# One transfer for the first tables, the last weights multiplied by the gate, and three idle products fewer in a two-layer hybrid kernel

## The chip, the cores and the metric

The kernel runs on one core of one Trainium2 chip. The metric is the device time of one execution in microseconds; a time stands for the median of several executions. The engines are named as the profile names them: PE (TensorE, matrix products; PEld are its weight loads), DVE (VectorE), ACT (ScalarE), POOL (GpSimd) and SP (SyncE, which issues most transfers). "ACTq" and "SPq" are transfers issued by ACT and SP.

## The reference

Two layers over 256 latent tokens of width 2048, with 256 context tokens as a prefix, all in fp32. The even layer mixes neighbourhood attention and a bidirectional Mamba-2 scan, the odd layer is a gated short convolution. Each layer modulates its normalised input by shift and scale and adds its output times a gate; the three come from the conditioning vector `c` (for the context rows from `c_ctx`) through `ada_w` and `ada_b`. Cut to what matters here:

```python
def adaln(cond, w, b):
    m = jax.nn.silu(cond) @ w + b
    return jnp.split(m, 3, axis=-1)                   # shift, scale, gate

def short_conv_mixer(h, w_in, conv_w, w_out):
    bg, cg, hv, g = jnp.split(h @ w_in, 4, axis=-1)
    return (jax.nn.silu(g) * (bg * dw_conv(cg * hv, conv_w))) @ w_out

for i in range(2):
    shift, scale, gate = adaln(c, ada_w[i], ada_b[i])
    h = rms_norm(x, norm_g[i]) * (1 + scale[:, None]) + shift[:, None]
    if i == 0:                                        # context rows too, with c_ctx
        y, _ = na_ssd_mixer(h, hc, ...)
    else:
        y = short_conv_mixer(h, sc_w_in[0], sc_conv_w[0], sc_w_out[0])
    x = x + gate[:, None] * y
return x
```

## The kernel before

**Numbers.** Every weight arrives in fp32 and is split into a high part (`split`: ACT copies it into an fp32r tile) and a low part (`low_part`: DVE subtracts the high part from the weight). A product of 128x128 by 128x512 is then three products: high by high, low by high, high by low. Activations are split in the same way (`hH`, `hL`; `y2` in the last product).

**Transfers.** A weight is a tile of 128x1024 (512 KB, `raw`), loaded by SP in the order of one list. `issue()` starts the next load when a `raw` buffer comes free. The small parameters lie in two tables, `small` and `const`, each with a first part (96 and 162 columns: conditioning vectors, norm weights and biases of layer 0; identity and a few constants) and a rest that is loaded later. ACT issues the two first parts at the program's start (L360, L362), ahead of everything else on its queue. SP issues the rows of `x` (L652), then the first weights of the modulation (L402).

**Order.** From about 60 us on, a planner sets the order by modelled times (`spawn`, `pump`, `force`: lists of tasks that yield until what they need is ready). The first part is another matter: `first()` holds a list of events, `at_(t, f)`, with times set by hand. The list is sorted by `t`, and its order is the order of the program on every engine.

**The head.** PE multiplies a tile of zeros (`warm(n, width)`, tile `tmp` at L204) while nothing is there to work on. ACT evaluates the tanh for SiLU of `c` and `c_ctx` (L548, `cth`), and ACT and DVE square the rows of `x` (L666, L668) for the norm. DVE and POOL make the factor (L640, L641), ACT and DVE scale the rows (L678), and PE turns the scaled rows (L209, `bank<-const,x`). Between them PE computes shift and scale of the first 256 channels: four products of 32x256 for each weight tile (`bank<-raw,cpad`, x8 in the profile, which counts two passes for a product in fp32; then `PT`, `xtm`, `yi`, which are spare places for weight tiles). `ada_copy` copies a result (`half`, L917), PE turns it (`bank<-const,half`), DVE makes `A` and `S` (L934, L936), ACT makes the modulated input `hH` (L1111), and the first product of the projections, that of K, follows (`bank<-w,hH`). Four idle products stand around the last pieces: `at_(18.97, warm, 1, 256)`, `at_(20.25, warm, 1, 256)`, `at_(20.72, warm, 1)` and `at_(20.73, warm, 1, 256)`. `r_turn` (`bank<-const,rx`) later turns the factors of the context rows, which arrive as `x<-in_cx`.

**The tail.** The last product is that of the odd layer, in four blocks of 512 columns. For each block `fin_gen` loads a row of the gate over all partitions (`tmp<-dram_mrow`), multiplies the result by it on DVE (L2575), adds the residual `x1` (L2578) and sends the block out (L2580). The last block is finished in three pieces, `LAST`: columns 0 to 256 of the second 128 tokens, then the first 128 tokens, then columns 256 to 512 of the second. The last six of its sixteen row blocks come from three weight tiles whose high and low parts lie in `KL`/`KL`, `QT`/`QL` and `wH`/`wL`; PE runs these six blocks piece by piece, after everything else.

Of the kernel before, what the change touches and what calls it, by code (L numbers as in the profile page):

```python
# [10 lines left out]
AF = mybir.ActivationFunctionType  # L11
# [4 lines left out]
KB = 16  # L16
# [4 lines left out]

_off = {}
_n = 0
for _name, _w in (("c", 16), ("cc", 16), ("g0", 16), ("ab0", 48), ("g1", 16), ("ab1", 48), ("cw", 160), ("cb", 32),
                  ("sg", 16), ("qg", 1), ("kg", 1), ("scw", 48), ("dtb", 1), ("alog", 1), ("dcol", 16)):
    _off[_name] = (_n, _n + _w)
    _n += _w
NSMALL, NFIRST = _n, 96
# [110 lines left out]


@with_exitstack
def kernel(ctx: ExitStack, tc, x, cx, ada0, w0, adaT, w_in, w_out, sc_in, sc_out, rpb, small, const,
                       strict, rows, scr, out):
    nc = tc.nc
    PS = bass.MemoryType.PSUM
# [9 lines left out]
    def st(shape, tag, dt=F32, name=None):  # L155
        return sb.tile(list(shape), dt, tag=tag, name=name or tag, bufs=1)
# [12 lines left out]
    WH = [t[:, :1024] for t in places]  # L169
    WL = [t[:, 1024:2048] for t in places]  # L170
    shifted = set()


    xrow = [st([128, D], "KT", name="x0")]
# [26 lines left out]
    def mm(o, l, r, start, stop):  # L201
        if start:
            bits[o.tensor.name] = o.shape[0] == 128 and o.shape[-1] == 512
        E(T.matmul(o, l, r, start=start, stop=stop, skip_group_check=True))  # L204
# [13 lines left out]
    def spawn(q, gen, tmps=0, halves=0, late=0):  # L218
        q.append(Task(gen, tmps, halves, late))
# [132 lines left out]
    def give(pool, *bs):  # L352
        pool.extend(bs)
# [2 lines left out]
    when = lambda f: ("if", f, 0)  # L356


    sm = st([128, NSMALL], "small")
    E(DMA2.dma_start(sm[:, :NFIRST], small[:, :NFIRST]))  # L360
    cs_ = st([128, NCONST], "const")
    E(DMA2.dma_start(cs_[:, :CFIRST], const[:, :CFIRST]))  # L362
# [59 lines left out]
    def split():  # L422
        k = pos["split"]
        raw, v = RAW.pop(k)
        nb, n = v.shape[1], v.shape[2]
        w = place()
        if n == 64:

            while lows:
                low_part()  # L430
            W = WH[w].rearrange("p (b c) -> p b c", b=nb)
            E(S.copy(W[:, :, :64], v))
            E(V.tensor_tensor(out=W[:, :, 64:], in0=v, in1=W[:, :, :64].bitcast(F32), op=ALU.subtract))
# [7 lines left out]
        E(S.copy(H, v))  # L441
        lows.append((k, H, Lo, v, raw))
        pos["split"] += 1
# [100 lines left out]
    zero = tmp()  # L544
    E(V.memset(zero, 0.0))
    E(V.memset(cpad, 0.0))
    cth = st([128, 32], "cth")
    E(S.activation(cth, sm[:, 0:32], AF.Tanh, scale=0.5))  # L548
    E(V.scalar_tensor_tensor(out=cth, in0=cth, scalar=1.0, in1=sm[:, 0:32], op0=ALU.add, op1=ALU.mult))
# [41 lines left out]
    for j in range(1, 7):  # L591
        q_w(j, 2)
        if j + 1 in DOTS:
            q_ada2(j + 1)
            q_dot(j + 1, 2)
            q_dot(j + 1, 3)
        else:
            q_ada(j + 1)
        q_w(j, 3)
        if j + 1 in DOTS:  # L600
            q_rowsA(j + 1)
        q_w(j, 4)
        if j == 3:
            loads.append(lambda: E(DMA.dma_start(sm[:, NFIRST:], small[:, NFIRST:])))
            loads.append(lambda: E(DMA.dma_start(cs_[:, CFIRST:], const[:, CFIRST:])))
        q_w(j + 1, 0)
        q_dot(j + 2, 0)
        q_w(j + 1, 1)
        q_dot(j + 2, 1)
# [113 lines left out]
    def chunk(kb0, kind, ps, first, last, lhs=None):  # L723

        H, Lo = use()
        nb = H.shape[1]
        for j in range(nb):
            kb = kb0 + j
            aH, aL = (hH[kb], hL[kb]) if lhs is None else lhs(kb)
            f, l = first and j == 0, last and j == nb - 1  # L730
            if kind == "act":
                mm_act(ps, aH, aL, H[:, j], Lo[:, j], f, l)
            else:
                mm_ws(ps, aH, aL, H[:, j], Lo[:, j], kind, f, l)
        used()
# [350 lines left out]
    def first():  # L1086
# [6 lines left out]
        def at_(t, f, *a):  # L1093
            ev.append((t + shift, len(ev), f, a))
# [1469 lines left out]
    def fin_gen(n, ps):  # L2564
        cols = slice(n * 512, (n + 1) * 512)
        yield when(lambda: n_back[0] >= 15)
        gb, os_ = tmp(), [tmp() for _ in range(2)]
        yield W_("SP", mrow[1:2])
        E(DMA.dma_start(gb, mrow[1, cols].partition_broadcast(128)))
        for t, c0, c1 in ((0, 0, 512), (1, 0, 512)) if n < 3 else LAST:  # L2570
            o = os_[t]
            c = slice(c0, c1)
            yield when(lambda: n < 3 or (3, t, c1) in at)
            yield W_("DVE", ps[t][:, c], gb)
            E(V.tensor_tensor(out=o[:, c], in0=ps[t][:, c], in1=gb[:, c], op=ALU.mult))  # L2575
            if c1 == 512:
                give(free_b, ps[t])
            E(V.tensor_tensor(out=o[:, c], in0=o[:, c], in1=x1[t][:, n * 512 + c0:n * 512 + c1], op=ALU.add))  # L2578
            yield W_("SP", o[:, c])
            E(DMA.dma_start(out[t * 128:(t + 1) * 128, n * 512 + c0:n * 512 + c1], o[:, c]))  # L2580
            if c1 == 512:
                give(free_t, o)
        give(free_t, gb)

    for n in range(4):
        if n == 1:
            force(lambda: n_back[0] >= 15, (urgent, back))
        ps = banks(2)
        for kb in range(0, KB if n < 3 else KB - 6, 2):
            force(lambda: y2[kb + 1] is not None)  # L2590
            chunk(kb, "act", ps, kb == 0, kb == KB - 2, lambda i: (y2[i][:, 0], y2[i][:, 1]))
        spawn(urgent, fin_gen(n, ps), 3)
# [12 lines left out]


_INS = ['x', 'cx', 'ada0', 'w0', 'adaT', 'w_in', 'w_out', 'sc_in', 'sc_out', 'rpb', 'small', 'const', 'strict', 'rows', 'scr']


# [73 lines left out]
```

## Time and profile before

| | us |
|---|---|
| median of 3 runs | 1724.89 |
| lowest, highest | 1723.09, 1725.05 |
| profiled execution, its own time | 1723.43 |
| its span | 1721.6 |

The span goes from the first to the last event of the profile; 1.8 us of the execution lie around it. The profile was taken from one execution on the one core, at a granted clock of 1.0. In rows of the timeline the numbers are the start and the duration in us; `x4` is a count; the bracket holds the idle time of the engine ahead of the row and what ended it. In rows of groups the numbers are the busy time in us and the mean of one instruction in ns.

### The profile page before, as it was taken

Reading aid. Unit: us, or ns where it says so; the run is one execution under the profiler, and the core shown is the slowest. Engines: PE = TensorE matmul, PEld = TensorE weight load, DVE = VectorE, ACT = ScalarE, POOL = GpSimd, SP = SyncE. Lnnn points to the kernel's source line nnn. Section 1 sums busy time; section 2 is a strip of 40 time slices with the busy share of each in tenths; the row PEclk is TensorE's granted clock in tenths of the full one; section 3 lists DMA queues with packets and bytes.
Section 4 is the critical chain, followed back from the end, with each engine's and each line's share of the span. In section 5 each row is a group of like instructions: output and inputs, shape, how many; then the busy total and the mean of one; then the engine's idle time right before and its main releaser. Section 6 shows DMA issues by size and latency. Waiting matters only on the chain.

```text
span 1721.6 us, 24689 instructions
## 1 busy us (share of the span) xinstructions
PE 1715.5 (100%) x9129; PEld 1449.9 (84%) x9129; DVE 1279.5 (74%) x2161; ACT 823.0 (48%) x1450; POOL 34.3 (2%) x28
## 2 busy tenths in 40 slices
PE   9999999999999999999999999999999999999999
PEld 5778899888889889889888898888888888888887
DVE  5699878877886778486877587887667767676754
ACT  6578464434553445244444244655444444444342
POOL 0000010000000000000001000000000000000000
PEclk9999999999999999999999999999999999999999
DMA  9988566456645675754775577767857788787863
GB/s 360 355 293 285 199 195 204 152 178 217 222 144 166 205 230 165 243 173 155 226 227 164 191 214 235 237 214 266 288 190 249 274 270 298 251 288 250 286 213 117
DMA packets 191368, 391.03 MB, mean 227 GB/s; under 512 B 16200, under 2 KB 45960, under 8 KB 190992
## 3 DMA queue, kind: packets, MB, share of 16 engines
q1 hardware_dynamic: 183936, 382.88, 67.2%
q10 hardware_dynamic: 7312, 6.59, 1.2%
q8 instruction: 71, 1.16, 0.3%
q14 instruction: 49, 0.40, 0.1%
HBM read 379.79 MB, written 9.62 MB: 226 GB/s over the span
## 4 chain that ended last, share of the span: by engine, by line
PE 99%; DMA 1%; DVE 0%; issue 0%
PE bank L204 96%; PE bank L209 3%; DMA raw<-in_ada 0%; DMA small<-in_small 0%; DVE tmp L2575 0%; DVE tmp L2578 0%
## 5 line engine op out<-in xcount | busy, mean ns | idle before, releaser
L441 ACT CAST w<-raw 128x1024 fp32r<-128x1024 f32 (+1 forms) x336 | 350.9, 1045 | 477.5 <-PE bank L204 389.2
L448 DVE TENSOR_TENSOR w<-raw,w 128x1024 fp32r<-128x1024 f32 (+1 forms) x336 | 406.9, 1215 | 215.0 <-ACT w L441 212.3
L204 PE MATMUL bank<-hH,w 128*128 128x256 f32 (+1 forms) x2064 | 486.5, 324 | 0.0
L204 PE MATMUL bank<-w,hH 128*128 128x512 f32 x1280 | 402.0, 394 | 0.0
L204 PEld LDWEIGHTS bank<-hH,w 128*128 128x128 f32 x2064 | 345.2, 188 | 32.1 <-issue 1.7
L204 PE MATMUL bank<-hL,w 128*128 128x256 f32 (+1 forms) x1040 | 334.7, 322 | 0.0
L204 PEld LDWEIGHTS bank<-w,hH 128*128 128x128 f32 x1280 | 236.9, 188 | 47.2 <-issue 0.8
L204 PE MATMUL bank<-w,hL 128*128 128x512 f32 x640 | 248.6, 391 | 0.0
L204 PEld LDWEIGHTS bank<-hL,w 128*128 128x128 f32 x1040 | 196.4, 189 | 14.5
L204 PE MATMUL bank<-w,h 128*128 128x512 f32 x768 | 178.5, 390 | 0.0
L204 PEld LDWEIGHTS bank<-w,h 128*128 128x128 f32 x768 | 144.0, 188 | 29.7
L842 DVE CUSTOM_DVE_ANT_0 raw<-raw,csb 128x1024 f32<-128x1024 f32 x128 | 155.3, 1219 | 10.5 <-DMA raw<-in_adaT 10.4
L204 PEld LDWEIGHTS bank<-w,hL 128*128 128x128 f32 x640 | 120.1, 188 | 25.3 <-DVE hL L1123 0.4
L204 PE MATMUL bank<-w,mix 128*128 128x512 f32 x588 | 138.4, 392 | 0.0
L204 PEld LDWEIGHTS bank<-w,mix 128*128 128x128 f32 x588 | 109.5, 188 | 22.0 <-issue 0.2
L204 PE MATMUL bank<-KL,h 128*128 128x512 f32 x264 | 63.6, 389 | 0.0
L1817 DVE SCALAR_TENSOR_TENSOR tmp<-bank,cwh,tmp 128x508 f32<-128x508 f32 (+1 forms) x80 | 59.4, 745 | 1.6
L204 PEld LDWEIGHTS bank<-KL,h 128*128 128x128 f32 x264 | 49.6, 188 | 10.3
L448 DVE TENSOR_TENSOR KL<-raw,KL 128x1024 fp32r<-128x1024 f32 x32 | 39.2, 1224 | 23.5 <-ACT KL L441 23.3
L204 PE MATMUL bank<-QT,h 128*128 128x512 f32 x168 | 55.8, 391 | 0.0
L204 PE MATMUL bank<-wH,h 128*128 128x512 f32 x168 | 55.3, 389 | 0.0
L441 ACT CAST QT<-raw 128x1024 fp32r<-128x1024 f32 x32 | 33.6, 1051 | 41.9 <-PE bank L204 34.5
(343 smaller groups left out, 2077.8 us busy)
## 6 DMA issues: line engine op xcount, KB each, us to landing
raw<-in_w_in SPq DMA_DIRECT2D x188, 512.0 KB, 3.7
raw<-in_adaT SPq DMA_DIRECT2D x128, 512.0 KB, 4.8
raw<-in_sc_in SPq DMA_DIRECT2D x128, 512.0 KB, 4.6
raw<-in_w_out SPq DMA_DIRECT2D x64, 512.0 KB, 4.6
raw<-in_ada SPq DMA_DIRECT2D x39, 512.0 KB, 6.2
raw<-in_sc_out SPq DMA_DIRECT2D x32, 512.0 KB, 4.5
tmp<-dram_csr SPq DMA_DIRECT2D x32, 256.0 KB, 5.8
raw<-in_w SPq DMA_DIRECT2D x15, 512.0 KB, 5.9
```

The source lines that it names most:

```text
L204: E(T.matmul(o, l, r, start=start, stop=stop, skip_group_check=True))
L209: E(T.transpose(o, i, ident if k == 128 else ident[:k, :k]))
L441: E(S.copy(H, v))
L448: E(V.tensor_tensor(out=Lo, in0=v, in1=H.bitcast(F32), op=ALU.subtract))
L842: E(V.tensor_tensor_reduce(out=raw, in0=raw, in1=csb, scale=1.0, scalar=0.0, op0=ALU.mult, op1=ALU.add, accum_out=gp[:, h, m:m + 1]))
L1817: E(V.scalar_tensor_tensor(out=do, in0=di, scalar=cwh[:, 32 * k + ch:32 * k + ch + 1], in1=do, op0=ALU.mult, op1=ALU.add))
```

## The change

There are three parts.

1. The two tables become one input, `tables`, ordered so that the two first parts lie side by side: 128 rows of 258 columns, 1032 bytes each, in place of 128 rows of 384 and 128 of 648 bytes. ACT issues that one transfer. Ahead of it ACT now runs a tanh on a tile of zeros, `cth`, which DVE clears first; the load of the function table stands in front of that tanh.
2. The gate of the last 512 columns is loaded once, ahead of the last three blocks of the loop (`gate3`). DVE multiplies the last three weight tiles by it, in place, before they are split. The last six row blocks then go into banks of their own (`last`) rather than on top of the ten before. `fin_gen` finishes the ten (gate and residual) as it finishes other blocks, and adds the banks of `last` piece by piece, with one addition for each.
3. Three of the four idle products around 20 us are left out; the 512 wide one stays.

```diff
+    tab = st([128, NSMALL + NCONST], "tables")
+    cth = st([128, 32], "cth")
+    sm, cs_ = tab[:, :NSMALL], tab[:, NSMALL:]
+    T0, T1 = NSMALL - NFIRST, NSMALL + CFIRST
+    E(V.memset(cth, 0.0))
+    E(S.activation(cth, cth, AF.Tanh))
+    E(DMA2.dma_start(tab[:, T0:T1], tables[:, T0:T1]))
-    sm = st([128, NSMALL], "small")
-    E(DMA2.dma_start(sm[:, :NFIRST], small[:, :NFIRST]))
-    cs_ = st([128, NCONST], "const")
-    E(DMA2.dma_start(cs_[:, :CFIRST], const[:, :CFIRST]))
...
+        if k >= nw[0] - 3:
+            E(V.tensor_tensor(out=v, in0=v, in1=gate3[0].unsqueeze(1).to_broadcast([128, 2, 512]), op=ALU.mult))
         E(S.copy(H, v))
...
-        at_(18.97, warm, 1, 256)
-        at_(20.25, warm, 1, 256)
         at_(20.72, warm, 1)
-        at_(20.73, warm, 1, 256)
...
+        for t in range(2):
             o = os_[t]
+            yield W_("DVE", ps[t], gb)
+            E(V.tensor_tensor(out=o, in0=ps[t], in1=gb, op=ALU.mult))
+            give(free_b, ps[t])
+            E(V.tensor_tensor(out=o, in0=o, in1=x1[t][:, cols], op=ALU.add))
+            if n < 3:
+                yield W_("SP", o)
+                E(DMA.dma_start(out[t * 128:(t + 1) * 128, cols], o))
...
+        for t, c0, c1 in LAST:
+            o, c = os_[t], slice(c0, c1)
+            yield when(lambda: (3, t, c1) in at)
+            yield W_("DVE", last[t][:, c], o)
+            E(V.tensor_tensor(out=o[:, c], in0=last[t][:, c], in1=o[:, c], op=ALU.add))
             yield W_("SP", o[:, c])
             E(DMA.dma_start(out[t * 128:(t + 1) * 128, n * 512 + c0:n * 512 + c1], o[:, c]))
...
         if n == 1:
             force(lambda: n_back[0] >= 15, (urgent, back))
+            force(lambda: budget[0] >= 1)
+            budget[0] -= 1
+            gate3.append(tmp())
+            E(DMA.dma_start(gate3[0], mrow[1, 1536:2048].partition_broadcast(128)))
...
+    last = banks(2)
     ws = [use(q) for q in range(3)]
     for t, c0, c1 in LAST:
         for q, (H, Lo) in enumerate(ws):
             for b in range(2):
                 hl = y2[KB - 6 + 2 * q + b]
                 for a_, w_ in ((0, H), (0, Lo), (1, H)):
-                    mm(ps[t][:, c0:c1], hl[:, a_, t * 128:(t + 1) * 128], w_[:, b, c0:c1], False, q == 2 and b == 1 and a_ == 1)
+                    st_ = q == 0 and b == 0 and a_ == 0 and w_ is H and c0 == 0
+                    mm(last[t][:, c0:c1], hl[:, a_, t * 128:(t + 1) * 128], w_[:, b, c0:c1], st_, q == 2 and b == 1 and a_ == 1)
```

What stands on the engines at the places that this moves follows, in the program's order. A name with a number is a tile, `[waits ...]` the semaphores that the instruction waits for.

On ACT, the program's first instructions before:

```order
L360 DMA small<-in_small 128x96
L362 DMA const<-in_const 128x162
L548 ACT_TABLE_LOAD
L548 ACTIVATE cth<-small 128x32 [waits DMAHW0_49]
L666 ACTIVATE tmp_66,ssq<-x_98 128x512 [waits DMAHW1_49]
```

and after:

```order
L365 ACT_TABLE_LOAD
L365 ACTIVATE cth<-cth 128x32 [waits DVE_49]
L366 DMA tables<-in_tables 128x258
L554 ACTIVATE cth<-tables 128x32 [waits DMAHW2_49,Activation_49]
L672 ACTIVATE tmp_66,ssq<-x_98 128x512 [waits DMAHW0_49]
```

The transfer has moved from the head of the queue to a place behind the table load and an activation that waits for DVE, and the activation on the tables waits for one transfer that holds both.

On PE, around the last pieces of the modulation (`xtm`, `yi`) and the first product of K, before:

```order
L204 MATMUL bank_86<-xtm,cpad 32x256 [waits DMAHW4_49]
L204 MATMUL bank_86<-xtm,cpad 32x256 x3
L204 MATMUL bank_84<-tmp_65 128x256 [waits DVE_49]
L204 MATMUL bank_86<-yi,cpad 32x256 [waits DMAHW5_49]
L204 MATMUL bank_86<-yi,cpad 32x256 x3
L204 MATMUL bank_85<-tmp_65 128x256 [waits DVE_49]
L209 MATMUL bank_86<-const,half_75 128x128 [waits Activation_49]
L209 MATMUL bank_86<-const,half_75 128x128
L204 MATMUL bank_87<-tmp_65 128x512 [waits DVE_49]
L204 MATMUL bank_88<-tmp_65 128x256 [waits DVE_49]
L204 MATMUL bank_89<-w_95,hH_308 128x512 [waits Activation_49]
```

and after:

```order
L205 MATMUL bank_86<-xtm,cpad 32x256 [waits DMAHW3_49]
L205 MATMUL bank_86<-xtm,cpad 32x256 x3
L205 MATMUL bank_86<-yi,cpad 32x256 [waits DMAHW4_49]
L205 MATMUL bank_86<-yi,cpad 32x256 x3
L210 MATMUL bank_86<-tables,half_75 128x128 [waits Activation_49]
L210 MATMUL bank_86<-tables,half_75 128x128
L205 MATMUL bank_84<-tmp_65 128x512 [waits DVE_49]
L205 MATMUL bank_85<-w_95,hH_305 128x512 [waits Activation_49]
```

The three idle products of 256 columns (`tmp_65` is the tile of zeros) are gone; the products on `yi` follow directly on those on `xtm`.

On DVE, the program's last instructions before (L448 is the low part of a weight, L2575 the gate, L2578 the residual):

```order
L448 TENSOR_TENSOR QL<-raw_91,QT 128x1024 [waits DMAHW7_49,Activation_49]
L448 TENSOR_TENSOR wL_9836<-raw_93,wH_9835 128x1024 [waits DMAHW0_49,Activation_49]
L2575 TENSOR_TENSOR tmp_71<-bank_82,tmp_66 128x256 [waits DMAHW4_49,PE_49]
L2578 TENSOR_TENSOR tmp_71<-tmp_71,x1b 128x256 [waits DVE_49]
L2575 TENSOR_TENSOR tmp_69<-bank_89,tmp_66 128x512 [waits PE_49]
L2578 TENSOR_TENSOR tmp_69<-tmp_69,x1a 128x512 [waits DVE_49]
L2575 TENSOR_TENSOR tmp_71<-bank_82,tmp_66 128x256 [waits PE_49]
L2578 TENSOR_TENSOR tmp_71<-tmp_71,x1b 128x256 [waits DVE_49]
```

and after (L446 is the multiplication of a weight by the gate, L454 the low part, L2578 the gate, L2580 the residual, L2592 the addition of a piece of the last six blocks):

```order
L446 TENSOR_TENSOR raw_91<-raw_91,tmp_65 128x1024 [waits DMAHW7_49]
L446 TENSOR_TENSOR raw_93<-raw_93,tmp_65 128x1024 [waits DMAHW0_49]
L454 TENSOR_TENSOR QL<-raw_91,QT 128x1024 [waits Activation_49]
L454 TENSOR_TENSOR wL_9833<-raw_93,wH_9832 128x1024 [waits Activation_49]
L2578 TENSOR_TENSOR tmp_69<-bank_85,tmp_65 128x512 [waits PE_49]
L2580 TENSOR_TENSOR tmp_69<-tmp_69,x1a 128x512 [waits DVE_49]
L2578 TENSOR_TENSOR tmp_71<-bank_82,tmp_65 128x512 [waits PE_49]
L2580 TENSOR_TENSOR tmp_71<-tmp_71,x1b 128x512 [waits DVE_49]
L2592 TENSOR_TENSOR tmp_71<-bank_86,tmp_71 128x256 [waits DVE_49,PE_49]
L2592 TENSOR_TENSOR tmp_69<-bank_87,tmp_69 128x512 [waits PE_49]
L2592 TENSOR_TENSOR tmp_71<-bank_86,tmp_71 128x256 [waits PE_49]
```

The multiplications by the gate stand ahead of the splits of the last weights, the first tile's a few rows earlier; behind the last product of PE one operation is left where two were.

More of the change, by code (lines that the diff above doesn't have):

```diff
@@ L23 @@
 _n = 0
-for _name, _w in (("c", 16), ("cc", 16), ("g0", 16), ("ab0", 48), ("g1", 16), ("ab1", 48), ("cw", 160), ("cb", 32),
-                  ("sg", 16), ("qg", 1), ("kg", 1), ("scw", 48), ("dtb", 1), ("alog", 1), ("dcol", 16)):
+for _name, _w in (("g1", 16), ("ab1", 48), ("cw", 160), ("cb", 32), ("sg", 16), ("qg", 1), ("kg", 1), ("scw", 48),
+                  ("dtb", 1), ("alog", 1), ("dcol", 16), ("c", 16), ("cc", 16), ("g0", 16), ("ab0", 48)):
     _off[_name] = (_n, _n + _w)
@@ L141, with kernel @@
 @with_exitstack
-def kernel(ctx: ExitStack, tc, x, cx, ada0, w0, adaT, w_in, w_out, sc_in, sc_out, rpb, small, const,
+def kernel(ctx: ExitStack, tc, x, cx, ada0, w0, adaT, w_in, w_out, sc_in, sc_out, rpb, tables,
                        strict, rows, scr, out):
@@ L171 @@
     shifted = set()
+    gate3 = []
     xrow = [st([128, D], "KT", name="x0")]
@@ L546 @@
     E(V.memset(cpad, 0.0))
-    cth = st([128, 32], "cth")
-    E(S.activation(cth, sm[:, 0:32], AF.Tanh, scale=0.5))
-    E(V.scalar_tensor_tensor(out=cth, in0=cth, scalar=1.0, in1=sm[:, 0:32], op0=ALU.add, op1=ALU.mult))
+    both = sm[:, _off["c"][0]:_off["cc"][1]]
+    E(S.activation(cth, both, AF.Tanh, scale=0.5))
+    E(V.scalar_tensor_tensor(out=cth, in0=cth, scalar=1.0, in1=both, op0=ALU.add, op1=ALU.mult))
     csil = st([128, 32], "csil")
@@ L603 @@
         if j == 3:
-            loads.append(lambda: E(DMA.dma_start(sm[:, NFIRST:], small[:, NFIRST:])))
-            loads.append(lambda: E(DMA.dma_start(cs_[:, CFIRST:], const[:, CFIRST:])))
+            loads.append(lambda: E(DMA.dma_start(tab[:, :T0], tables[:, :T0])))
+            loads.append(lambda: E(DMA.dma_start(tab[:, T1:], tables[:, T1:])))
         q_w(j + 1, 0)
@@ L2566, in fin_gen @@
         yield when(lambda: n_back[0] >= 15)
[L2567 to L2570, printed above, removed]
-            o = os_[t]
[L2572 to L2578, printed above, removed]
+        gb = tmp() if n < 3 else gate3[0]
+        os_ = [tmp() for _ in range(2)]
+        if n < 3:
+            yield W_("SP", mrow[1:2])
+            E(DMA.dma_start(gb, mrow[1, cols].partition_broadcast(128)))
+        for t in range(2):
+            o = os_[t]
+            yield W_("DVE", ps[t], gb)
+            E(V.tensor_tensor(out=o, in0=ps[t], in1=gb, op=ALU.mult))
+            give(free_b, ps[t])
+            E(V.tensor_tensor(out=o, in0=o, in1=x1[t][:, cols], op=ALU.add))
+            if n < 3:
+                yield W_("SP", o)
+                E(DMA.dma_start(out[t * 128:(t + 1) * 128, cols], o))
+                give(free_t, o)
+        if n < 3:
+            give(free_t, gb)
+            return
+        for t, c0, c1 in LAST:
[3 more added lines that the diff above has]
+            E(V.tensor_tensor(out=o[:, c], in0=last[t][:, c], in1=o[:, c], op=ALU.add))
             yield W_("SP", o[:, c])
             E(DMA.dma_start(out[t * 128:(t + 1) * 128, n * 512 + c0:n * 512 + c1], o[:, c]))
-            if c1 == 512:
-                give(free_t, o)
-        give(free_t, gb)
     for n in range(4):
@@ L2587 @@
             force(lambda: n_back[0] >= 15, (urgent, back))
+            force(lambda: budget[0] >= 1)
+            budget[0] -= 1
+            gate3.append(tmp())
+            E(DMA.dma_start(gate3[0], mrow[1, 1536:2048].partition_broadcast(128)))
         ps = banks(2)
-        for kb in range(0, KB if n < 3 else KB - 6, 2):
+        k1 = KB if n < 3 else KB - 6
+        for kb in range(0, k1, 2):
             force(lambda: y2[kb + 1] is not None)
-            chunk(kb, "act", ps, kb == 0, kb == KB - 2, lambda i: (y2[i][:, 0], y2[i][:, 1]))
-        spawn(urgent, fin_gen(n, ps), 3)
+            chunk(kb, "act", ps, kb == 0, kb == k1 - 2, lambda i: (y2[i][:, 0], y2[i][:, 1]))
+        spawn(urgent, fin_gen(n, ps), 3 if n < 3 else 2)
+    last = banks(2)
     ws = [use(q) for q in range(3)]
@@ L2604 @@
     force(lambda: not urgent, (urgent,))
-_INS = ['x', 'cx', 'ada0', 'w0', 'adaT', 'w_in', 'w_out', 'sc_in', 'sc_out', 'rpb', 'small', 'const', 'strict', 'rows', 'scr']
+_INS = ['x', 'cx', 'ada0', 'w0', 'adaT', 'w_in', 'w_out', 'sc_in', 'sc_out', 'rpb', 'tables', 'strict', 'rows', 'scr']
 def kernel(**inputs):
@@ L2668 @@
         'w_out': f('na_ssd_w_out')[0], 'sc_in': f('sc_w_in')[0], 'sc_out': f('sc_w_out')[0], 'rpb': table,
-        'small': small, 'const': const, 'strict': strict,
+        'tables': np.concatenate([small, const], axis=1), 'strict': strict,
         'rows': np.concatenate([f('ssd_dt_bias')[0].reshape(1, 64), f('ssd_a_log')[0].reshape(1, 64)], axis=1),
```

7 lines of the change are left out of this document (3 added, 4 removed).

## The prediction

> **What bounds the kernel now.** I read the page first: the busy times, the clock row and the chain that ended last. Then the list of everything that TensorE (PE) waited for.
>
> ```profile
> PE 1715.5 (100%) x9129; PEld 1449.9 (84%) x9129; DVE 1279.5 (74%) x2161; ACT 823.0 (48%) x1450; POOL 34.3 (2%) x28
> ...
> PEclk9999999999999999999999999999999999999999
> ...
> PE 99%; DMA 1%; DVE 0%; issue 0%
> ```
>
> ```profile
> PE bank L204 <- DVE tmp L545: 1.5, 1, 1.5
> PE bank L204 <- DVE rx L640: 1.0, 1, 1.0
> ```
>
> PE is busy for 1715.5 of 1721.6 us, at full clock in every slice, and 99% of the chain is PE. Its only waits that the list shows are 1.5 us for the first zero tile and 1.0 us ahead of its first real product. All of that is over by 11 us. From there PE works without a break, so time taken from or given to PE in the head is carried to the end, unless a later input holds PE at a fixed time. Two places can therefore matter: the head, up to about 35 us, and what comes after the last product. Everything between is the same rows in the same order, with PE as its limit.
>
> **The tail: one operation instead of two behind the last product.** These rows of the timeline are the end of the program and what lies ahead of it (start, duration, engine, what, and in brackets the idle time before it and who ended it).
>
> ```profile
> 1702.53 1.23 DVE L448 TENSOR_TENSOR wL<-raw,wH 128x1024 fp32r<-128x1024 f32 x1 [1.24 <-ACT wH L441]
> ...
> 1709.41 0.88 PE L204 MATMUL bank<-KL,y 128*128 128x256 f32 x6
> ...
> 1711.76 0.42 DVE L2575 TENSOR_TENSOR tmp<-bank,tmp 128x256 f32<-128x256 f32 x1 [8.00 <-PE bank L204]
> ...
> 1717.70 0.28 PE L204 MATMUL bank<-wH,y 128*128 128x256 f32 x1
> 1718.02 0.42 DVE L2575 TENSOR_TENSOR tmp<-bank,tmp 128x256 f32<-128x256 f32 x1 [0.73 <-PE bank L204]
> 1718.47 0.43 DVE L2578 TENSOR_TENSOR tmp<-tmp,x1b 128x256 f32<-128x256 f32 x1
> ```
>
> Before, the last product ends at 1717.98, the multiplication by the gate starts at 1718.02, the addition at 1718.47, and the output leaves behind it. Afterwards one addition of the same 128x256 stands there, since the gate is in the weights and the sum so far already lies in SBUF. What goes is the step from one start to the next, 1718.47 - 1718.02 = **0.45 us**. What is late next is the same product of PE, so nothing takes the operation's place.
>
> What pays for it: three multiplications of 128x1024 on DVE, each priced by the low part of the same shape, 1.23 us; and two full-width pairs on the banks as they stand before the last six blocks (four operations of 128x512, some 0.7 us each, between the 0.42 of 128x256 and the 1.23 of 128x1024). DVE has been idle for 8.00 us ahead of 1711.76. The multiplications, 3 x 1.23 = 3.7 us, go into that hole and delay the casts behind them: per block at most the multiplication and the low part waiting behind it. The last low part starts at 1702.53 before, and PE takes the first of these blocks at 1709.41, 5.6 us after 1703.76. With all 3.7 us in a row ahead of the last block, 1.9 us are still left. The four partial operations start when PE closes the earlier blocks, at about 1709.6, take 2.9 us and end near 1712.6, while the last product is 5 us later. I cost all of this at **nothing**. Without that cover it would cost up to 3.7 us. The gate row is now loaded once, earlier, on SP's queue, 40 us ahead of its use; the load of 256 KB is the same one, moved.
>
> **The head: three idle products.** First the transfer on which the next real product waits (issue, KB, median us to landing), then the timeline from the first idle product on.
>
> ```profile
> yi<-in_ada SPq DMA_DIRECT2D x1, 512.0 KB, 10.2
> ```
>
> ```profile
> 9.36 0.33 SPq L402 DMA_DIRECT2D yi<-in_ada  x1
> ...
> 18.95 0.64 PE L204 MATMUL bank<-xtm,cpad 128*32 128x256 f32 x8
> 19.52 0.70 PE L204 MATMUL bank<-tmp 128*128 128x256 f32 x2
> 20.15 0.64 PE L204 MATMUL bank<-yi,cpad 128*32 128x256 f32 x8
> ...
> 20.85 0.37 ACT L917 COPY half<-bank 128x256 f32<-128x256 f32 x1 [1.43 <-PE bank L204]
> ...
> 21.28 0.44 PE L209 MATMUL bank<-const,half 128*128 128x128 f32 x2
> 21.55 1.46 PE L204 MATMUL bank<-tmp 128*128 128x512 f32 x4
> ...
> 22.29 1.09 ACT L1111 ACTIVATE hH<-xm,S,A 128x256 fp32r<-128x256 f32 x2 [0.54 <-DVE S L936]
> ...
> 22.94 0.74 PE L204 MATMUL bank<-w,hH 128*128 128x512 f32 x2
> ...
> 33.00 0.32 PE L209 MATMUL bank<-const,rx 128*128 128x128 f32 x1
> ```
>
> The first idle product stands at 19.52 and holds back the products on yi until 20.15, 0.63 us. yi lands at 9.36 + 10.2 = 19.56. Without the idle product they start at about 19.6, 0.5 us earlier. The second one, behind yi's products, hides: the turn at 21.28 waits for ScalarE's copy of the bank (20.85 + 0.37 = 21.22) in any case. The third hides in the same way with the part of the row at 21.55 that is left: the first product of K at 22.94 needs hH, whose ACT row starts at 22.29. So the copy, the turn, S, hH and the first product of K move by 0.5 us together, to about 22.4, and two of the three products bring nothing of their own.
>
> How much of the 0.5 us is left further on? DVE squares a quarter of the context rows, which come with the DMA stream and do not move:
>
> ```profile
> 24.72 0.68 DVE L668 CUSTOM_DVE_ANT_0 tmp<-x 128x512 f32<-128x512 f32 x1
> 25.33 0.69 DVE L469 TENSOR_TENSOR w<-PT,w 128x512 fp32r<-128x512 f32 x1
> 28.51 0.69 DVE L668 CUSTOM_DVE_ANT_0 tmp<-x 128x512 f32<-128x512 f32 x1 [0.29 <-DMA x<-in_cx]
> ```
>
> The low half of K at 25.33 stands behind that square and so can move by little; 28.51 waits for the stream outright, and the turn at 33.00 is a fixed time later, behind DVE's and GpSimd's work on those sums. K's low product, and then 33.00, take back what PE was ahead by. Its bounds are 0 (everything taken back) and -0.5 us (nothing). I take **-0.2 us**, nearer to 0, since the row at 28.51 shows that the chain to 33.00 hangs on the transfer.
>
> **The tables as one transfer.** Here the trace does not show the new thing: a DMA issued by ScalarE (ACT) behind its table load.
>
> ```profile
> 0.73 0.41 ACTq L360 DMA_DIRECT2D small<-in_small  x1
> ...
> 1.17 0.46 ACTq L362 DMA_DIRECT2D const<-in_const  x1
> ...
> 1.67 1.28 ACT L548 ACT_TABLE_LOAD   x1 [1.67 <-PEq L2672]
> ...
> 5.10 0.23 ACT L548 ACTIVATE cth<-small 128x32 f32<-128x32 f32 x1 [2.15 <-DMA small<-in_small]
> ...
> 8.09 0.69 DVE L668 CUSTOM_DVE_ANT_0 tmp<-x 128x512 f32<-128x512 f32 x1 [0.29 <-DMA x<-in_x]
> ...
> 11.31 1.33 ACT L678 ACTIVATE x<-x,rx 128x512 f32<-128x512 f32 x2 [0.61 <-POOL rx L641]
> ...
> 12.53 0.66 PE L209 MATMUL bank<-const,x 128*128 128x128 f32 x4
> ```
>
> ```profile
> 288.92 1.05 ACT L441 CAST w<-raw 128x1024 fp32r<-128x1024 f32 x1 [1.39 <-issue]
> 288.94 0.79 ACTq L1801 DMA_DIRECT2D dram_csr<-tmp  x2
> ```
>
> The table load costs 1.28 us and hides before and after; the small activation on zeros adds 0.23. What can cost time is the landing. small is issued at 0.73 and lands 4.37 us later, when the activation at 5.10 starts. If ACT's sequencer issues past a running operation, as at 288.94 under the cast of 288.92, tables leave at about 1.1 and land near 1.1 + 4.37 = 5.5, 0.4 late. If the load and the activation block it, they leave at 0.73 + 1.28 + 0.23 = 2.24 and land near 6.6, 1.5 late. What queues behind: ACT's first squares stand behind the activation that waits for tables, and so do DVE's, behind the two operations on cth; the scaled rows of the second block and their turn on PE stand behind those. There is room: 0.29 us of idle time ahead of DVE's square at 8.09, and the scaled quarter is done at 11.31 + 0.67 = 11.98, 0.55 ahead of its turn at 12.53. So 0.84 us are free. The delays are **0** for a landing 0.4 late and 1.5 - 0.84 = 0.66 us for one 1.5 late, and that falls on the stretch that has just lost a 0.63 us idle product: the head gain goes first. Below nothing there is a little too: the rows of x share the engines with one queue of 128 pieces less. The two transfers hold 48 + 81 KB, which at 512 KB in 1.27 us (raw tiles: PE took two of them at 11.96 and 13.23) is 0.3 us of bytes; I bound the gain at 0.2. I take 0, nearest to the row at 288.94.
>
> ```profile
> 11.96 0.64 PE L204 MATMUL bank<-raw,cpad 128*32 128x256 f32 x8
> ...
> 13.23 0.64 PE L204 MATMUL bank<-raw,cpad 128*32 128x256 f32 x8
> ```
>
> The Trainium skill, in "ScalarE: Activation LUTs", section "What ACT_TABLE_LOAD costs", speaks against this part: it gives about 1283 ns for the load, which the row at 1.67 bears out, and about 1380 ns of drain behind it, 2.66 us in all. The trace of before cannot show the drain, since the activation behind the load waits for small until 5.10. By that page the tables would leave at 0.73 + 2.66 = 3.4 us; the term would then be about +1.8 rather than 0 (an estimate from that page's figure, with small's 4.37 us to landing).
>
> **Sum.** Tail -0.45, head -0.2, tables 0: **-0.65 us**, bounds -0.45 - 0.5 - 0.2 = -1.15 and, with the head gain lost, -0.45. On the profiled execution that is 1723.43 - 0.65 = 1722.8. The median of the runs shown is 1724.89, 1.46 above that execution, and the runs spread over 2 us; put on the median, it is **1724.2**.
>
> **Rivals.**
> - *The tables land late and hold PE* (the slower side). Place: the turn at 12.53. Point: a landing more than 0.84 us after 5.10. For it: no row shows an issue behind a table load. Against it: 288.94. With the landing 1.5 late the 0.66 us eat the 0.63 of the idle product and the rest is the tail, 1724.4. Slower than before it becomes from a landing about 1.9 late on (0.84 + 0.63 + 0.45). If the operation behind the load starts only after a pause as long as the load (1.28 more), the landing is 2.8 late: 2.8 - 1.9 = +0.9 us, 1725.8. The skill's drain, named above, is of that kind.
> - *PE falls back to its slow start.* The windows of the head show what that is:
>
> ```profile
> 0.00:7.40 7.40, 5.95 (x7) 2.53 (x8) 2.89 (x11) 2.85 (x6) 0.20 (x4) 1.00 0.69 232
> 7.40:10.70 3.30, 2.40 (x6) 0.76 (x4) 2.73 (x10) 2.61 (x6) 0.55 (x1) 1.00 1.02 416
> ```
>
>   One pass of the same idle product (fp32 takes two) is 5.95 / 7 = 0.85 us up to 7.4 and 2.40 / 6 = 0.40 behind it. If the thinner work between 19.5 and 22.9 sent PE back for as long a stretch, seven passes would lose 0.45 us each, 3.1 us, and with the tail 1724.89 + 3.1 - 0.65 = 1727.3. Against it: PE stood still for 1.0 us (the list of waits) before its first real product, and those at 11.96 then took the same 0.64 as at 18.95. The new gaps are near 0.4 and 0.5 us, and a 512-wide idle product stays between them. The Trainium skill, "TensorE: Matmul & The Clock Gate", Part 1, puts the return to half speed behind an idle window of about 3.4 us; by it the loss would be none here, and 1.7 us if it came.
> - *It does not do what it says in the head*: K's low half and the turn at 33.00 take back all, so -0.45 alone, 1724.4.
> - *The stream runs ahead*: nothing is taken back and x lands earlier, -1.15, 1723.7.
>
> **Chances and range.** Forecast 0.50, nothing left in the head 0.20, late tables 0.17, stream ahead 0.10, slow PE 0.03. The range: the lowest run with the lower bound, 1723.09 - 1.15 = 1721.9, and the highest run with the late tables, 1725.05 + 0.9 = 1725.9. About 0.2%, 3.4 us, is what a measurement of this kernel can tell from no change; no case but a long slow stretch or a shifted run reaches it: faster 0.02, same 0.95, slower 0.03.
>
> **What would show it.** Right: in the timeline's tail one operation between the last product and the output, with the start of the second one gone; the products on yi at about 19.6 with no idle product ahead; the first product of K near 22.4; the turn that stood at 33.00 within 0.5 us of it; the DMA row of tables at 1.1 and the first activation on it before 5.9. Wrong: the activation on tables after 6.0 with the turn of 12.53 later than that; PE waits for KL, QT or wH at the end, which would mean that the multiplications are not hidden; passes of 512 columns above 0.8 us after 20 us; or a span that differs by more than 3 us, which none of these terms could give.

## The result, and the profile after

| | us |
|---|---|
| median after (4 runs) | 1761.46 (1760.65 to 1762.46) |
| median before, all runs beside them (4) | 1724.22 |
| ratio | 1.0215, 95% interval 1.0203 to 1.0228 |
| profiled execution after, its own time and span | 1760.65, 1758.9 |

The change makes the kernel slower by 37 us. The forecast was 0.7 faster, and none of its cases reached this. The page of the changed kernel answers to the first lines of the prediction, and the list of PE's waits to the second fence:

```profile
PE 1751.5 (100%) x9123; PEld 1451.2 (83%) x9123; DVE 1284.5 (73%) x2166; ACT 823.2 (47%) x1451; POOL 33.4 (2%) x28
...
PEclk9999999999999999999999999999999999999999
...
PE 99%; DMA 1%; SPq 0%; ACT 0%; DVE 0%; issue 0%; DVEq 0%; ACTq 0%
```

```profile
PE bank L205 <- DVE rx L646: 1.7, 1, 1.7
PE bank L205 <- DVE tmp L551: 1.5, 1, 1.5
PE bank L210 <- ACT half L923: 0.5, 1, 0.5
PE bank L205 <- ACT hH L1117: 0.4, 1, 0.4
```

PE has six records fewer and is busy for 36 us longer. Its waits have grown by less than 2 us, all of it in the head, and the granted clock is full in every slice. So PE did not wait for more: the same products took longer. Where? The chain of waits holds stretches with the same 112 products. Three of them before and after (start, duration, what):

```profile
107.67 23.02 PE bank L204 x112
130.92 23.02 PE bank L204 x112
154.16 23.02 PE bank L204 x112
```

```profile
108.72 23.59 PE bank L205 x112
132.53 23.59 PE bank L205 x112
156.34 23.58 PE bank L205 x112
```

A stretch takes 23.59 instead of 23.02 us, 2.5% more, and this goes on to the end. The groups by line and shape tell which products they are (busy us, mean ns of one); before:

```profile
L204 PE MATMUL bank<-w,h 128*128 128x512 f32 x768 | 178.5, 390 | 0.0
L204 PE MATMUL bank<-KL,h 128*128 128x512 f32 x264 | 63.6, 389 | 0.0
L204 PE MATMUL bank<-hH,w 128*128 128x256 f32 x1280 | 232.8, 282 | 0.0
L209 PE MATMUL bank<-const,tmp 128*128 128x128 f32 x308 | 43.4, 272 | 0.0
```

and after:

```profile
L205 PE MATMUL bank<-w,h 128*128 128x512 f32 x768 | 183.5, 395 | 0.0
L205 PE MATMUL bank<-KL,h 128*128 128x512 f32 x264 | 65.3, 395 | 0.0
L205 PE MATMUL bank<-hH,w 128*128 128x256 f32 x1280 | 237.0, 283 | 0.0
L210 PE MATMUL bank<-tables,tmp 128*128 128x128 f32 x308 | 43.4, 272 | 0.0
```

The first name behind the arrow is the operand that streams, the second the one that is loaded into the array; the view prints fp32r and plain fp32 both as f32. Products in fp32r, of weights with the split activations, take longer; those in plain fp32 (`const,tmp`, 43.4 us) do not. In the trace the time from the start of one `w,h` product to the start of the next is 227.1 ns before and 233.7 ns after (means over 743 neighbouring pairs). Summed over the traces from each product's start to the next, the 5806 products of 512 columns other than the idle ones take 34.1 us more (5.9 ns each on average) and the 1920 of 256 columns with `hH` or `hL` take 4.2 us more (2.2 ns each). That is 38.3 us; the first product of K starts 0.5 us earlier (22.40 against 22.94) and the stretch behind the last product is 0.4 us shorter, which leaves the 37.3 us by which the span has grown.

What had changed for these products? Not their order: from the first product of K to the last product, the traces of before and after hold the same 9009 records of PE in the same order. Their place had changed. Tiles lie one behind the other in SBUF, each rounded up to 32 bytes. `small` held 436 columns of 4 bytes, 1744, rounded 1760; `const` 610 columns, 2440, rounded 2464; together 4224. `tables` holds 1046 columns, 4184, rounded 4192: 32 bytes less. The compiled programs list these places (bytes within a partition):

```
tile                      before     after
w0 (weight parts)          48256     48256
KL                         98176     98176
small / tables            130944    130944
hH0 (also mix0, y2_0)     184192    184160
hL0 (also h1_0)           188288    188256
VH                        222048    222016
```

The activations' tiles, and almost everything else behind the tables, have moved down by 32 bytes against the weights' tiles, which lie ahead of them. (The exceptions are `cth`, which now lies right behind the tables, and the tile of `cpad` and `v`, which moved up by 96 to make room for it; no row of the tables above reads them.)

### The profile page after: what moved, and what is told of

Read it like the earlier page. It is cut to its first block, busy times and chain, and to the rows that moved or that the text cites. A ratio compares the mean times of both kernels' runs of the same rounds, so it can differ in the third digit from the quotient of the medians.

```text
span 1758.9 us, 24679 instructions
## 1 busy us (share of the span) xinstructions
PE 1751.5 (100%) x9123; PEld 1451.2 (83%) x9123; DVE 1284.5 (73%) x2166; ACT 823.2 (47%) x1451; POOL 33.4 (2%) x28
## 4 chain that ended last, share of the span: by engine, by line
PE 99%; DMA 1%; SPq 0%; ACT 0%; DVE 0%; issue 0%; DVEq 0%; ACTq 0%
PE bank L205 96%; PE bank L210 3%; DMA raw<-in_ada 1%; SPq L658 0%; SPq L406 0%; ACT hH L1117 0%; DVE tmp L2592 0%; ACT half L923 0%; DVE S L940 0%; DVE S L942 0%; DVEq L940 0%; ACTq L1117 0%
## 5 line engine op out<-in xcount | busy, mean ns | idle before, releaser
L454 DVE TENSOR_TENSOR w<-raw,w 128x1024 fp32r<-128x1024 f32 (+1 forms) x336 | 406.9, 1214 | 238.3 <-ACT w L447 236.9
L205 PE MATMUL bank<-hH,w 128*128 128x256 f32 (+1 forms) x2064 | 494.7, 327 | 0.0
L205 PE MATMUL bank<-w,hH 128*128 128x512 f32 x1280 | 408.7, 399 | 0.4 <-ACT hH L1117 0.4
L205 PE MATMUL bank<-w,h 128*128 128x512 f32 x768 | 183.5, 395 | 0.0
L205 PEld LDWEIGHTS bank<-w,hL 128*128 128x128 f32 x640 | 119.9, 188 | 29.0 <-DVE hL L1129 0.4
L205 PEld LDWEIGHTS bank<-KL,h 128*128 128x128 f32 x264 | 49.5, 187 | 12.1
L454 DVE TENSOR_TENSOR KL<-raw,KL 128x1024 fp32r<-128x1024 f32 x32 | 39.2, 1224 | 26.7 <-ACT KL L447 26.6
L454 DVE TENSOR_TENSOR QL<-raw,QT 128x1024 fp32r<-128x1024 f32 x32 | 39.1, 1223 | 21.6 <-ACT QT L447 21.3
```

Of the source, the lines that this page charges most:

```text
L454: E(V.tensor_tensor(out=Lo, in0=v, in1=H.bitcast(F32), op=ALU.subtract))
```

## The experiments

**Theory A**: the place makes the products slow. **Theory B**: something in the new order does (the other banks, the missing idle products). The first run moves the activations' tiles back to where they were and leaves every instruction as it is in the changed kernel.

*e1: the 32 bytes given back.*

```diff
-    cth = st([128, 32], "cth")
+    cth = st([128, 40], "cth")[:, :32]
```

> The changed kernel with one tile 32 bytes wider behind the tables; every instruction the same, but all tiles allocated behind it (the inputs hH and hL of the products, h, mix, y) are back at the addresses they had in the kernel before, multiples of 64 bytes. Theory A (place in memory: 32 bytes off a multiple of 64 makes every fp32r product slower, 227 to 234 ns for 512 columns): 1723.6 us, 0.65 below before, spacing 227. Theory B (the new order, the banks or the missing idle products slow PE): 1761 us, as the change, spacing 234.

Measured: 1722.89 us, ratio to before 0.9996 (0.9987 to 1.0006). A holds, B falls. `w,h` stands at 227.1 ns from start to start again:

```profile
L205 PE MATMUL bank<-w,h 128*128 128x512 f32 x768 | 178.5, 389 | 0.0
L205 PE MATMUL bank<-KL,h 128*128 128x512 f32 x264 | 63.6, 389 | 0.0
```

*e2: the kernel before, pushed by 32 bytes.*

```diff
-    sm = st([128, NSMALL], "small")
+    sm = st([128, NSMALL + 8], "small")[:, :NSMALL]
```

> The kernel before with the table small 32 bytes wider; every instruction the same, the tiles behind it 32 bytes off a multiple of 64. Theory A: about 1724 + 37 = 1761 us, spacing 234 ns for 512 columns of fp32r. Theory B: 1724 us, spacing 227.

Measured: 1762.78 us, ratio 1.0223 (1.0206 to 1.0241). None of the change's edits is in it, and it is as slow as the change.

*e3: the changed kernel, pushed by 96 bytes; e4: the kernel before with the weights moved by 32 bytes instead.*

```diff
-    cth = st([128, 32], "cth")
+    cth = st([128, 56], "cth")[:, :32]
...
-    WH = [t[:, :1024] for t in places]
-    WL = [t[:, 1024:2048] for t in places]
+    WH = [t[:, 8:1032] for t in places]
+    WL = [t[:, 1032:2056] for t in places]
```

> The changed kernel with a tile 96 bytes wider: the tiles behind it at an odd multiple of 64 bytes, where before had multiples of 128. If the unit is 64 bytes: 1723.6 us, as with 32 bytes. If it is 128 bytes: 1761 us or between. Theory B: 1761 us.

> The kernel before with the high and low parts of the weights in the three tiles w moved by 32 bytes inside their tiles; hH, hL and all else stay on multiples of 64. Theory A, if it holds for either operand of a product: the products with w at 233 to 235 ns, those with KL, QT and wH at 227; about 1724 + 5000/5600 x 37 = 1757 us at most. If only the operand of the activations counts (hH, h, y as the place that the change moved): 1724 us. Theory B: 1724 us.

Measured: 1759.89 us (ratio 1.0209, 1.0189 to 1.0230) and 1750.89 us (1.0157, 1.0137 to 1.0178). So multiples of 64 bytes are not enough, and for `w,h` it is all the same which operand moves: 233.7 ns from start to start in both runs. That leaves two readings: **M**, each operand has to lie on a multiple of something larger, or **R**, only the distance between the two counts. e5 and e7 move both operands by the same amount, e6 and e8 look for the unit and the grain.

*e5 to e8.* e5: the edits of e2 and of e4 together. e6 and e8: the edit of e4 with 32 and with 4 columns (128 and 16 bytes) in place of 8. e7: the edit of e3, with the weights moved by 16 columns (64 bytes):

```diff
-    WH = [t[:, :1024] for t in places]
-    WL = [t[:, 1024:2048] for t in places]
+    WH = [t[:, 16:1040] for t in places]
+    WL = [t[:, 1040:2064] for t in places]
```

> The kernel before with the tiles behind small (hH, hL, h, mix, y) 32 bytes off and the parts of the weights in w 32 bytes off as well; KL, QT and wH stay. Theory R (only the distance between the two operands counts, modulo 128 bytes): products of w with h, hH, mix or y at 227 ns again, those of KL, QT, wH with h or y at 233; some 1000 of them x 6.6 ns = 6.6 us, and the 256 column products as in the run with the tiles alone 32 off, 1900 x 1.9 ns = 3.6 us: about 1734 us. Theory M (each operand has to lie on a multiple of 128 bytes): all at 233 or more, 1761 us or above.

> The kernel before with the parts of the weights in w moved by 128 bytes. If the unit is 128 bytes, by R and by M: 1724 us, 227 ns. If it is 256 bytes or more: 233 ns with w, 1751 us, as with 32 bytes.

> The changed kernel with the tiles behind the tables at an odd multiple of 64 bytes and the parts of the weights in w at one as well; KL, QT and wH stay. R: products of w with h at 227 ns, KL with h at 233, the 256 column products as in the run with 96 bytes (119.9 against 116.7 ns, 6 us): about 1737 us. M: 1760 us.

> The kernel before with the parts of the weights in w moved by 16 bytes. If what counts is a grain of 32 bytes or more: 1724 us, 227 ns. If any distance counts: 233 to 235 ns with w, about 1751 us, as with 32 bytes.

Measured: 1736.23, 1747.88, 1739.42 and 1743.52 us (ratios 1.0073, 1.0135, 1.0086 and 1.0110, the intervals of all four at 1.005 or above). The groups of e5 and then of e7, where the distance between `w` and `h` is that of before, but neither lies where it lay:

```profile
L204 PE MATMUL bank<-w,h 128*128 128x512 f32 x768 | 179.0, 390 | 0.0
L204 PE MATMUL bank<-KL,h 128*128 128x512 f32 x264 | 65.3, 396 | 0.0
L204 PE MATMUL bank<-hH,w 128*128 128x256 f32 x1280 | 236.8, 283 | 0.0
```

```profile
L205 PE MATMUL bank<-w,h 128*128 128x512 f32 x768 | 178.9, 390 | 0.0
L205 PE MATMUL bank<-KL,h 128*128 128x512 f32 x264 | 65.3, 394 | 0.0
L205 PE MATMUL bank<-hH,w 128*128 128x256 f32 x1280 | 239.6, 285 | 0.0
```

`w,h` is fast again in both, while `KL,h`, where only `h` has moved, stays slow in the same execution. R holds and M falls. For e6 and e8:

```profile
L204 PE MATMUL bank<-w,h 128*128 128x512 f32 x768 | 183.3, 395 | 0.0
```

```profile
L204 PE MATMUL bank<-w,h 128*128 128x512 f32 x768 | 182.2, 394 | 0.0
```

128 bytes are as bad as 32, so the unit is not the 128 that the expectation of e5 had assumed; 16 bytes already cost most of it. In the kernel before all these operands lie 128 beyond a multiple of 256; w0 at 48256 and the next weight tile at 56704 differ by 256 modulo 512, and both are fast. So a unit of 256 fits all these runs.

| run | streamed minus loaded, `w,h`, bytes modulo 256 | start to start, ns |
|---|---|---|
| before, e1 | 0 | 227.1 |
| e5, e7 | 0, both moved by 32, by 64 | 227.8, 227.7 |
| e8 | 16 | 231.9 |
| after, e4 | 32 | 233.7 |
| e6 | 128 | 233.5 |
| e3 | -64 | 233.7 |
| e2 | -32 | 233.6 |

A smaller thing remains: `KL,h` takes 228 to 230 ns on average in e4, e6 and e8, where neither of its operands has moved. The traces show where that sits. In e4 the twelve products of `KL,h` that begin at 1317.6 us, behind products of `w,h` at 233.7 ns, stand 241, 224, 231, 235, 229, 232 and 231 ns apart, and from there on 226 or 227; `QT,h` behind them is at 227. In e5, where the products of `KL`, `QT` and `wH` take the 233 ns, those of `w,h` behind them begin with 230, 236, 229, 232 and 231 ns and then fall to 226 or 227, which is why e5 and e7 stand at 227.8 and 227.7 in the table and not at 227.1. So the longer time carries over into the next few products, whatever their own distance. Why it does is open.

Open is also which loaded operand counts. In these stretches a load starts 2 to 4 ns after the start of a product and takes 188 ns, so it most likely fetches the operand of the next product while this one streams. All the activations' tiles lie alike modulo 256, so no run tells whether the product's own operand counts or the next one's.

*e9: the three idle products back, with the 32 bytes.*

```diff
+        at_(18.97, warm, 1, 256)
+        at_(20.25, warm, 1, 256)
         at_(20.72, warm, 1)
+        at_(20.73, warm, 1, 256)
```

> The changed kernel with the 32 bytes, and the three idle products put back. If the head gain is what the first idle product held back: the products on yi at about 20.15 again, 0.5 later than in the run with the 32 bytes alone, the first product of K near 22.9, the turn that stood at 33.00 within 0.1 of it; the time about 0.25 us above that run, which no comparison can tell. If the tables or the stream made the gain: the products on yi at 19.6 to 19.7 plus the idle product's length hidden, and no difference at 33.

Measured: 1723.10 us, ratio to before 0.9995 (0.9984 to 1.0005), which its time cannot tell from e1. The timeline of e9 shows the head gain undone; e1's follows it:

```profile
20.21 0.64 PE L205 MATMUL bank<-yi,cpad 128*32 128x256 f32 x8
...
23.01 0.73 PE L205 MATMUL bank<-w,hH 128*128 128x512 f32 x2
...
33.19 0.32 PE L210 MATMUL bank<-tables,rx 128*128 128x128 f32 x1
```

```profile
19.67 0.64 PE L205 MATMUL bank<-yi,cpad 128*32 128x256 f32 x8
20.80 0.44 PE L210 MATMUL bank<-tables,half 128*128 128x128 f32 x2 [0.49 <-ACT half L923]
21.08 1.02 PE L205 MATMUL bank<-tmp 128*128 128x512 f32 x2
22.46 0.73 PE L205 MATMUL bank<-w,hH 128*128 128x512 f32 x2 [0.36 <-ACT hH L1117]
...
32.77 0.32 PE L210 MATMUL bank<-tables,rx 128*128 128x128 f32 x1
```

The products on `yi` come 0.54 us earlier without the idle products, and 0.42 of it is left at the turn of the factors. Against before (33.00) e1 is ahead by 0.23.

*e10: VH and VL at a distance of 0 from P.* Theory R, applied to products that it had not been tried on. The 32 bytes of e1 are in this run and in e11 and e12 as well.

```diff
-    gqk = st([128, 1], "gqk")
+    gqk = st([128, 9], "gqk")[:, :1]
```

> The changed kernel with the 32 bytes, and one small tile 32 bytes wider ahead of VH and VL, so that their distance from P, the other operand, is a multiple of 256 bytes. Theory R: 64 products of up to 512 columns and 64 shorter ones lose up to 6.6 ns each, 0.5 us at most: 1722.4 us, not to be told from the run with the 32 bytes by the time.

Measured: 1723.58 us, ratio 0.9993 (0.9983 to 1.0003); the gain was not to be seen in the time in any case, but it is not in the groups either. Before and e10:

```profile
L204 PE MATMUL bank<-P,VH 128*128 128x512 f32 x32 | 12.1, 399 | 0.0
```

```profile
L205 PE MATMUL bank<-P,VH 128*128 128x512 f32 x32 | 12.0, 399 | 0.0
```

The distance does nothing that these groups show. 12.1 us for 32 of them is 378 ns each, not 227: these products do not follow one another closely. That this is the reason is not shown.

*e11 and e12: the products of 256 columns.* Their weights already lay 64 bytes into their tiles before (`shifted`), while those of the 512 column products lie at 0. Here the activations stream and the weights are loaded.

```diff
-        H, Lo = (places[w][:, 16:1040], places[w][:, 1040:2064]) if k in shifted else (WH[w], WL[w])
+        H, Lo = (places[w][:, 32:1056], places[w][:, 1056:2080]) if k in shifted else (WH[w], WL[w])
...
+        H, Lo = (places[w][:, 48:1072], places[w][:, 1072:2096]) if k in shifted else (WH[w], WL[w])
```

> The changed kernel with the 32 bytes; the weights of the 1920 products of 256 columns, which lie 64 bytes into their tiles, at 128 bytes instead. These products took 116.7 ns at a distance of 64 bytes and 119.9 at 0. If 128 is as for 512 columns, one distance among the bad ones: 119 ns, +4 us, 1727. If the best distance is half the unit of 256: below 116 ns, down to 113 (their lowest tenth), -6 us, 1717.

> As the run before, at 192 bytes, 64 below the next multiple of 256. If only the size of the distance counts: as with 64 bytes, 116.7 ns, 1723. If its sign counts: between 118 and 120 ns, 1726 to 1729.

Measured: 1729.51 us (1.0031, 1.0020 to 1.0042) and 1726.27 us (1.0011, 1.0001 to 1.0021). e11 and e12:

```profile
L205 PE MATMUL bank<-hH,w 128*128 128x256 f32 x1280 | 238.5, 284 | 0.0
```

```profile
L205 PE MATMUL bank<-hH,w 128*128 128x256 f32 x1280 | 235.2, 281 | 0.5 <-DVE w L454 0.5
```

Both are worse than the 232.8 of before at 64 bytes, and e3 and e7 at a distance of 0 are the worst with 239.6. From start to start, `hH,w` takes 116.7 ns before, with the weights 64 bytes above the activations modulo 256 (115.7 to 116.5 in the other runs that leave this distance alone), 118.5 or 118.6 at 32 and 96, 119.9 or 120.0 at 0 and 128, and 117.8 at 192. So short products have another best distance than long ones, and half the unit is not the answer. The sign counts only a little (117.8 against 116.7), and in e12 PE also waited 0.5 us for DVE there. Of the distances tried the one in the kernel is the best. No version beats the kernel before by more than the measurement can tell: e1, e9 and e10, which have the change's rows with the tiles moved back, lie 0.04 to 0.07% below it, and each interval holds 1.

## Why the prediction was wrong

**The step that failed** is in the first part: "Everything between is the same rows in the same order, with PE as its limit." The rows are the same, PE is the limit, and nothing waits; I took from it that each row takes as long as before. It does not: a product of `w,h` takes 233.7 ns from start to start instead of 227.1, and all the fp32r products of 512 and 256 columns together take 38.3 us more. The term was missing from the sum, on the longest stretch of the kernel, where I had looked for waits alone. A merged tile was counted as a transfer, a landing and a queue, never as a place in SBUF. The last line of the prediction's signs, "a span that differs by more than 3 us, which none of these terms could give", is what came.

The Trainium skill, "TensorE: Matmul & The Clock Gate", Part 2, "Step-by-step: what each phase is for", says that PE has two independent read ports and that "Loading the next tile's weights doesn't steal SBUF read bandwidth from the running matmul." That speaks for no such term. The runs differ: for fp32r products of 512 columns back to back, the distance between the streamed and the loaded operand changes the time of one by 2.9% (233.7 / 227.1). That the two reads get into each other's way inside SBUF would fit a cost that hangs on their distance, but no run shows it; it stays an inference. The record of a load itself stays at 187 or 188 ns whichever of the two times a product takes.

**The other terms**, read from e1, which has the change without the shift:

- *Tail*, -0.45. The end of the program in e1, then the page's span:

```profile
1716.82 0.28 PE L205 MATMUL bank<-wH,y 128*128 128x256 f32 x1
1717.14 0.42 DVE L2592 TENSOR_TENSOR tmp<-bank,tmp 128x256 f32<-128x256 f32 x1 [1.46 <-PE bank L205]
```

```profile
span 1720.3 us, 24679 instructions
```

  One operation stands behind the last product. From its end at 1717.10 to the end of the span it is 3.2 us, against 1721.6 - 1717.98 = 3.6 before: -0.4. The multiplications are hidden, as forecast; in the changed kernel DVE is idle for 4.17 us behind them:

```profile
1737.61 2.35 DVE L446 TENSOR_TENSOR raw<-raw,tmp 128x1024 f32<-128x1024 f32 x2
1740.03 1.22 DVE L454 TENSOR_TENSOR QL<-raw,QT 128x1024 fp32r<-128x1024 f32 x1
1741.17 1.22 DVE L454 TENSOR_TENSOR wL<-raw,wH 128x1024 fp32r<-128x1024 f32 x1
1746.56 0.69 DVE L2578 TENSOR_TENSOR tmp<-bank,tmp 128x512 f32<-128x512 f32 x1 [4.17 <-PE bank L205]
```

- *Head*, -0.2. The products on `yi` at 19.67 (forecast 19.6), K at 22.46 (22.4), 0.23 ahead of before at the turn of 33.00. e9 gives 0.42 for the idle products alone; its own head runs 0.06 to 0.19 behind that of before. The size came out as forecast, but the reason for choosing it did not: the turn of the factors follows the product ahead of it by 11 ns in e1, so no fixed time held it. Product by product against before, e1 is 0.49 us ahead at 25.63 and 0.28 at 26.75. Two products there start 300 and 340 ns after the ones ahead of them, where DVE has the low half of K ready at 25.88 (25.19 + 0.69), only 0.14 earlier than before. The forecast had named that place too, but took its number from the other.
- *Tables*, 0. ACT's first rows in the changed kernel:

```profile
0.73 1.28 ACT L365 ACT_TABLE_LOAD   x1 [0.73 <-PEq L2689]
0.94 0.40 ACTq L366 DMA_DIRECT2D tables<-in_tables  x1
2.02 0.23 ACT L365 ACTIVATE cth<-cth 128x32 f32<-128x32 f32 x1
5.18 0.23 ACT L554 ACTIVATE cth<-tables 128x32 f32<-128x32 f32 x1 [2.92 <-DMA tables<-in_tables]
```

  The transfer leaves at 0.94, during the table load, and lands 0.08 later than `small` did, well inside the 0.84 us of room (in e1 the activation on the tables starts at 5.14, 0.04 later than before). The rival of late tables falls. So does, for this load, the drain that the Trainium skill, "ScalarE: Activation LUTs", section "What ACT_TABLE_LOAD costs", puts behind a table load: the activation starts 0.01 us after the load's end.
- *The slow start of PE* did not come back: with the idle products left out, as in e1, the products run at 227.1 ns.

Sum of these from e1: its profiled execution is 1722.13 us against 1723.43, -1.3, of which the tail and the head give -0.65; the other 0.65 builds up between 130 and 610 us, mostly over products of 256 columns, whose time from start to start hops between 113 and 119 ns in both (means 116.7 before, 116.3 in e1). No term of the forecast speaks of that part. By the medians the difference is 1722.89 against 1723.68, -0.8. That this comes near the -0.65 of the sum is partly luck: the interval of the ratio holds 1, so the time alone shows neither a gain nor its absence, and what confirms the tail and the head are their rows. The forecast described the change as it would be with its tiles where they were.

## What to carry to other kernels

When an edit changes the size or the order of any tile, compare the addresses of the operands that PE streams and loads, not only the order of the instructions: here a merged table shifted the activations' tiles behind it by 32 bytes and cost 37 us, and eight spare columns brought them back. In this kernel fp32r products of 512 columns, back to back, are fastest with the streamed and the loaded operand at a distance that is a multiple of 256 bytes; those of 256 columns are fastest, of the distances tried, at one of 64 bytes. If PE is busy for longer at the same number of products and full clock, look at the time from start to start of one product, by shape and by data type, before looking for waits.

## What was not expected of the hardware

The rate of a product hangs on the distance between two operands that are read from different tiles: 227.1 ns at 0, 231.9 at 16 bytes, 233.5 to 233.7 at 32 to 128. Behind a stretch at 233.7 ns the next few products still take longer although their own distance is 0: up to 241 ns in e4, before they are at 226 or 227. The plain fp32 products `const,tmp` show nothing of it (43.4 or 43.5 us for 308 in every run, with the table moved by 16 or 32 bytes), and neither do the fp32r products `P,VH`, which do not follow one another closely (12.0 to 12.2 us for 32). A DMA issued by ScalarE went out 0.21 us after the start of a table load of 1.28 us, and an activation of the same queue started right at the load's end.
